# One pool of 80 for the tiles of layer B, and the silu'd gates kept in DRAM

## The chip, the core and the metric

The kernel runs on one core of a Trainium2 chip. The metric is the device time of one execution in microseconds (us), taken as the median of several runs. Besides the times there is one profiled execution, from which the hardware profiler recorded each engine's instructions. The engines are TensorE (PE, with its weight loads shown apart as PEld), VectorE (DVE), ScalarE (ACT), GpSimd (POOL) and SyncE (SP), whose queue issues the DMAs. On-chip memory is SBUF (the working memory, 128 partitions) and PSUM (the accumulators of TensorE).

## What is computed

A trunk of two layers on 512 positions of width 2048, all in float32, and between them a shared key and value side.

```python
def pool_mixer_layer(x, norm_g, w_in, w_group, scale, w_out):      # layer A
    proj = rmsnorm(x, norm_g) @ w_in
    u, gate = proj[..., :W_A], proj[..., W_A:]                     # W_A = 4096, 4 groups
    pooled = [causal_mean_pool(u_g, w) - u_g for w in (2, 4, 8, 16)]
    y = einsum('bsgc,gcd->bsgd', pooled, w_group) * scale * silu(gate)
    return x + y @ w_out

def shared_kv(x, ...):                                             # 512 latents -> 16 heads
    c, k_rope = split(rmsnorm(x, kv_norm_g) @ kv_w_a)
    k_nope, v = split(rmsnorm(c, kv_latent_g) @ kv_w_b)
    return qk_norm_rope([k_nope, k_rope]), v

def mla_layer(x, k, v, ...):                                       # layer B
    q_lat, gate = split(rmsnorm(x, norm_g) @ w_in)                 # gate: 16 heads x 128
    q = qk_norm_rope(rmsnorm(q_lat, q_latent_g) @ w_q_b)
    o = chunk_causal_attention(q, k, v)                            # softmax, causal by chunks of 64
    return x + (o * silu(gate)) @ w_out
```

## The kernel before

The activations are stored transposed: a tile is 128 channels by 512 positions in float32, 2 KB in each partition. To keep float32 accuracy each operand of a product is split into a high part (rounded to the matmul's own format, on ACT) and a low part (the rest, on DVE), and a product is three matmuls, hi x hi, hi x lo and lo x hi (`mm3`, L139 to L143). `load_w` (L114) loads a 128 x 512 weight block from SP's queue into `raw`, and makes `whi` (ACT, L123) and `wlo` (DVE, L124); four of each exist. `proj` (L127) runs one output tile: for 16 inputs, four blocks of weights and 48 matmuls. `split` (L145) makes hi (L146) and lo (L147) of an activation tile.

The stages, in the order of the code:

1. Layer A's input projection, by a scheme of seven products in place of eight (matmuls at L325 to L329). `gather` (L332) adds up the results in a tile `e` and stores them to DRAM scratch (L346, L348). Its memory (the x parts, the weight parts, `e` and small tiles) is given back at the end of the stage.
2. Layer A's rest (L422 to L457). For each of 4 groups `g`: eight pooled tiles, loaded from scratch and split (`pooled_tile`, hi and lo by `at`); eight `y_tile`s (a product with `awg`, hi and lo by `bt`); sixteen products with `awo`, added to the 16 residual tiles `xr` at L455. The residual tiles come from `xt` and are loaded after the y tiles of g = 0 (L450).
3. The norm's gains and the splits of the 16 residual tiles, once for the shared side (`xkv`, from `at`) and once for layer B (`xb`, from `bt`); each residual tile is then spilled to DRAM.
4. The latents: four tiles `cl` from `xt`, the rotary key, the normed `cn` (eight `at` tiles); then the query latents `ql` (four `xt`, evicted from PSUM at L488) and `qn` (eight `at`).
5. The 16 gates, one unit each (`gate_unit`, L568): a `proj` over `xb`, times the norm (L572), then silu into an `at` tile (L574) that is held until its head is done. Gates 0 to 11 come first, then the preparation of head group 0, then gates 12 to 15.
6. The attention, 8 groups of 2 heads. `attn_units` lists a group's work: `score_unit` (matmuls at L731, mask, max at L736, exp at L739), `pt_unit` (transposes of the probabilities, split into `xt` tiles), `pv_unit` (the products with v at L775 to L777, and after a head's second one the gate's product at L780, `V.tensor_tensor(gt, ov, gt, ALU.mult)`). Between them a list of "fill" work is woven, the preparation of the next group, in the order of `PREP`:

```python
PREP = "B k0 k1 k2 k3 K q0 q1 T0 T2 q2 T1 q3 T3 T4 S T5".split()
```

   B loads weights and takes tiles; k0 to k3 are the key and value products (L605 to L607; keys copied at L609); K and S are the statistics of keys and queries (S at L659 to L661 and on); q0 to q3 are the query products (L625 to L627, evicted at L630); T0 to T5 are transposes (L701) followed by splits (T5 ends at L706 and L707, the others in `split`). Due times decide which fill unit stands ahead of which unit of attention (`LEAD`, `PACE`).
7. The output: for the last group, the fill work is `og_unit` (the gated heads are split into `at` or `bt` tiles) and `out_unit` (products with `bwo`). At the end `out_store` loads each spilled tile into an `xt` tile, adds the product and stores the result.

Three pools of SBUF carry the tiles of stages 2 to 7: 32 buffers for `at`, 32 for `bt`, 16 for `xt`, side by side in this order behind the weight buffers. Because `bt` tiles run short in the first head group, its v tiles and two of its transposed pairs are taken from `xt` instead (L591, L710). PSUM has three banks for products (`mm`), two for scores, two for transposes and one for the attention's output. Inside each pool the buffers are handed out in the order of the code; the order in which one engine executes its instructions is chosen by a scheduler, which takes what is ready, and the earlier in the code first.

Of the kernel before, what the change touches and what calls it, by code (L numbers as in the profile page):

```python
# [7 lines left out]
F32 = mybir.dt.float32  # L8
F32R = mybir.dt.float32r
I32 = mybir.dt.int32  # L10
AF = mybir.ActivationFunctionType
# [3 lines left out]
P = 128  # L15
S = 512
# [35 lines left out]
def trunk_kernel(  # L52
# [16 lines left out]
    nc = tc.nc  # L69
    V, A, G, T = nc.vector, nc.scalar, nc.gpsimd, nc.tensor  # L70
# [4 lines left out]
    dpool = ctx.enter_context(tc.tile_pool(name="dpool", bufs=16, space=bass.MemoryType.DRAM))  # L75

    def xt(shape=(P, S), dt=F32):
        return xpool.tile(list(shape), dt, tag="x", name="xt")

    def at(dt=F32R):  # L80
        return apool.tile([P, S], dt, tag="a", name="at")

    def bt(shape=(P, S), dt=F32R):
        return bpool.tile(list(shape), dt, tag="b", name="bt")

    ca = ExitStack()
    tp = [None]
# [1 line left out]
    def tt_(n=S, dt=F32):  # L89
        return tp[0].tile([P, n], dt, tag="t", name="tt_")  # L90
# [4 lines left out]
    def sc():  # L95
        return ps.tile([P, S], F32, tag="sc", name="sc", bufs=2)
# [30 lines left out]
    def proj(w, nk, xs, m=P, acc=None):  # L127

        acc = acc or mm()
        c = S // m if m == P else 4  # L130
        for k0 in range(0, nk, c):
            hi, lo = load_w(w[:, k0 * m:(k0 + c) * m], c * m)
            for j in range(c):
                k = k0 + j
                mm3(acc[:m, :], hi[:, j * m:(j + 1) * m], lo[:, j * m:(j + 1) * m], xs[k],
                    k == 0, k == nk - 1)
        return acc
# [90 lines left out]
    tile_ = dict(reuse_waits="tile")  # L228
# [31 lines left out]
    with ExitStack() as c1:  # L260
# [91 lines left out]
        with ExitStack() as c2:  # L352
            hp = c2.enter_context(tc.tile_pool(name="hp", bufs=2, **tile_))
            for j in range(NJ):
# [11 lines left out]
                a, b = xh[j], xl[j]  # L366
# [43 lines left out]
            gather(ks, pair)  # L410

    wpool = ctx.enter_context(tc.tile_pool(name="wpool", bufs=3, **tile_))
    apool = ctx.enter_context(tc.tile_pool(name="apool", bufs=32, **tile_))
    bpool = ctx.enter_context(tc.tile_pool(name="bpool", bufs=32, **tile_))
    xpool = ctx.enter_context(tc.tile_pool(name="xpool", bufs=16, **tile_))
    tp[0] = ca.enter_context(tc.tile_pool(name="tpool2", bufs=6, **tile_))
    ps = ctx.enter_context(tc.tile_pool(name="ps", bufs=2, space=bass.MemoryType.PSUM, **tile_))

# [3 lines left out]
    def pooled_tile(g, o):  # L422
        x = tt_()
        nc.sync.dma_start(x, raws[g * 8 + o])
        if g:
            x = pool_tile(x, g * 8 + o in neg, WINS[g])
        hi, lo = at(), at()
        split(x, hi, lo)
        return hi, lo

    def y_tile(g, o, pooled):
        z = tt_()
        nc.sync.dma_start(z, raws[32 + g * 8 + o])
        V.scalar_tensor_tensor(z, z, -1.0 if 32 + g * 8 + o in neg else 1.0, ra[0], ALU.mult, ALU.mult)
        A.activation(z, z, AF.Silu)
        acc2 = proj(awg[g, o], 8, pooled)
        c = C_ASC + g * 8 + o
        V.scalar_tensor_tensor(z, acc2, cs[:, c:c + 1], z, ALU.mult, ALU.mult)
        hi, lo = bt(), bt()
        split(z, hi, lo)  # L440
        return hi, lo

    pooled = [pooled_tile(0, o) for o in range(8)]
    for g in range(NG):
        ys = [y_tile(g, o, pooled) for o in range(8)]
        if g == 0:
            rope_tables()
            for k in range(KD):
                x = xt()
                nc.sync.dma_start(x, xT[k])  # L450
                xr.append(x)
        pooled = []
        for o in range(KD):
            acc = proj(awo[g, o], 8, ys)
            V.tensor_tensor(xr[o], xr[o], acc, ALU.add)  # L455
            if g + 1 < NG and o % 2:
                pooled.append(pooled_tile(g + 1, o // 2))  # L457
# [6 lines left out]
    for k in range(KD):  # L464
        hi, lo = at(), at()
        gsplit(xr[k], C_GKV + k, hi, lo)
        xkv.append((hi, lo))
        hi, lo = bt(), bt()
        gsplit(xr[k], C_GB + k, hi, lo)
        xb.append((hi, lo))  # L470
        if k < 2:
            A.activation(accs[k], xr[k], AF.Square)
        else:
            sq = tt_()
            A.activation(sq, xr[k], AF.Square)
            V.tensor_tensor(accs[k % 2], accs[k % 2], sq, ALU.add)
        dsp = dpool.tile([P, S], F32, tag="dsp", name="dsp")
        nc.sync.dma_start(dsp, xr[k])
        spill.append(dsp)
# [10 lines left out]
    def latent_norm(lat, gcol):  # L490
        ac = tt_()
        A.activation(ac, lat[0], AF.Square)
        for o in range(1, 4):
            sq = tt_()
            A.activation(sq, lat[o], AF.Square)
            V.tensor_tensor(ac, ac, sq, ALU.add)
        r = norm_r(ac, 512)
        res = []
        for o in range(4):
            V.scalar_tensor_tensor(lat[o], lat[o], cs[:, gcol + o:gcol + o + 1], r, ALU.mult, ALU.mult)  # L500
            hi, lo = at(), at()
            split(lat[o], hi, lo)
            res.append((hi, lo))
        return res

    cl = []
    for o in range(4):
        c = xt()
        latent(wkvc[o], o, xkv, c)
        cl.append(c)  # L510
# [50 lines left out]
    for o in range(4):  # L561
        c = xt()
        latent(bwin[o], o, xb, c)
        ql.append(c)
    qn = latent_norm(ql, C_GQL)

    gates = []

    def gate_unit(o):
        acc = proj(bwin[4 + o], KD, xb)  # L570
        z = tt_()
        V.tensor_tensor(z, acc, rb[0], ALU.mult)  # L572
        sg = at(F32)
        A.activation(sg, z, AF.Silu)  # L574
        gates.append(sg)


    gqk = const.tile([P, 1], F32, name="gqk")
# [4 lines left out]
    def small(n=8, tag="sm", bufs=6):  # L583
        return spool.tile([P, n], F32, tag=tag, name=tag, bufs=bufs)
# [93 lines left out]
    def tr_unit(hg, u):  # L678

        d = st[hg]  # L680
        if u == 2:


            d["kr"] = []
            for h in range(2):
                p = tr()
                for t in range(4):
                    T.transpose(p[:, t * P:(t + 1) * P], d["krs"][h][:, t * P:(t + 1) * P], ident)
                kh, kl = (xt(dt=F32R) if h else rpool.tile([P, S], F32R, tag="r", name="kr0")), bt()
                split(p, kh, kl)  # L690
                d["kr"].append((kh, kl))
            return
# [25 lines left out]

    def score_unit(hg, h, i):
        d = st[hg]  # L720
        n = (i + 1) * P
        s = sc()
        kh, kl = d[("T", h)]
        krh, krl = d["kr"][h]
        qh, ql_ = d[("T", 3 + h)]
        qr = d["qr"][h]
        qs = slice(i * P, (i + 1) * P)
        ops = [(qh[:, qs], kh[:, 0:n]), (qh[:, qs], kl[:, 0:n]), (ql_[:, qs], kh[:, 0:n]),
               (qr[:, qs], krh[:, 0:n]), (qr[:, qs], krl[:, 0:n])]
        for j, (l, r) in enumerate(ops):  # L730
            T.matmul(s[:, 0:n], l, r, start=(j == 0), stop=(j == 4))  # L731
        V.memset(s[0:64, n - 64:n], -1e30)
        nm = small(1, "nm", 4)
        V.tensor_reduce(nm, s[:, 0:n], AX.X, ALU.max)
        rq = d["rq"][:, 2 * i + h:2 * i + h + 1]
        V.scalar_tensor_tensor(nm, nm, -1.0, rq, ALU.mult, ALU.mult)  # L736
        pe = tt_()
        sm = small(1, "sm", 4)
        A.activation(pe[:, 0:n], s[:, 0:n], AF.Exp, bias=nm, scale=rq, accum_out=sm)  # L739
        V.reciprocal(sm, sm)  # L740
        V.tensor_scalar(pe[:, 0:n], pe[:, 0:n], sm, None, ALU.mult)
        d[("P", h, i)] = pe
# [52 lines left out]
    def attn_units(hg):  # L795
        seq = [(h, i) for h in range(2) for i in range(4)]
        res = []

        for n in range(len(seq) + 2):
            if n < len(seq):  # L800
                res.append(lambda n=n: score_unit(hg, *seq[n]))
            if n >= 2:
                h, i = seq[n - 2]
                res.append(lambda h=h, i=i: pt_unit(hg, h, i))
                if i % 2:
                    res.append(lambda h=h, i=i: pv_unit(hg, h, i // 2))
        return res
# [28 lines left out]
    for o in range(12):  # L836
        gate_unit(o)
    for u in prep_units(0):
        u()
    for o in range(12, NH):  # L840
        gate_unit(o)
# [98 lines left out]
```

## Time and profile before

| what | before |
| --- | --- |
| median of 3 runs | 1957.51 us (1957.45 to 1959.82) |
| profiled execution | 1954.67 us |
| its span, first to last instruction | 1952.5 us |
| mean granted TensorE clock | 0.999 |
| HBM read and written | 208.35 MB, 25.17 MB |

The lines of the profile name an engine, a line of the kernel, an operation and "output <- inputs" by the program's names, with a count of instructions and times in us. "Busy" is the time in which an engine executes something. An idle time in brackets, as in `[0.73 <-ACT whi L123]`, is followed by what ended it: here the ACT instruction at L123 that wrote `whi`. A row of the table by stage gives a stretch of the span, its length, the busy time (and count) of PE, PEld, DVE, ACT and POOL, the clock that TensorE was granted (1.00 is full speed), the share of the DMA engines' time in use, and GB/s.

### The profile page before, as it was taken

To read this page: it belongs to the slowest core of one execution; us is meant where nothing else is said; L and a number is where in the kernel's file an instruction comes from. 1 tells how busy PE (TensorE), PEld (TensorE's weight loads), DVE (VectorE), ACT (ScalarE), POOL (GpSimd) and SP (SyncE) were. 2 spreads that over 40 slices of the span, in tenths; PEclk is the share of its full clock that TensorE was granted. 3 is DMA by queue.
4 is the path that set the end of the run, shared out by engine and by line. 5 is a ranking of instruction groups with operands and counts; after the bars stand their busy time and mean duration, and the time that the engine had idled before them with its cause. 6 is when DMAs were issued, how large, how long until landed. Compare 5 with 4: busy or idle time off the path is not lost.

```text
span 1952.5 us, 30593 instructions
## 1 busy us (share of the span) xinstructions
PE 1920.2 (98%) x11356; PEld 1708.7 (88%) x11356; DVE 1275.8 (65%) x2289; ACT 820.5 (42%) x1561; POOL 264.8 (14%) x404
## 2 busy tenths in 40 slices
PE   8999999999999999999999999999999999999999
PEld 7899999999999878888888888888888888888887
DVE  8766676797666587486695567473344788797432
ACT  7533333333333443333333454332244777785221
POOL 0442323344322100000000000000010111110000
PEclk9999999999999999999999999999999999999999
DMA  6644344335444465334344343333322111121632
GB/s 199 202 135 140 119 138 133 125 125 173 136 124 131 154 212 159 113 121 143 114 130 130 119 146 124 92 92 97 98 92 76 56 39 53 45 70 48 218 119 87
DMA packets 168133, 235.52 MB, mean 121 GB/s; under 512 B 14896, under 2 KB 95152, under 8 KB 167984
## 3 DMA queue, kind: packets, MB, share of 16 engines
q1 hardware_dynamic: 167696, 233.37, 38.0%
q8 instruction: 89, 1.46, 0.3%
q14 instruction: 60, 0.49, 0.1%
q10 hardware_dynamic: 288, 0.20, 0.0%
HBM read 208.35 MB, written 25.17 MB: 120 GB/s over the span
## 4 chain that ended last, share of the span: by engine, by line
PE 91%; DVE 4%; ACT 2%; DMA 1%; issue 1%; SPq 0%; DVEq 0%; ACTq 0%
PE mm L143 16%; PE mm L141 16%; PE mm L142 16%; PE k L329 9%; PE k L325 9%; PE k L327 9%; PE sc L731 2%; PE mm L605 2%; PE mm L607 1%; PE mm L606 1%; PE mm L625 1%; DVE lo L309 1%; PE mm L626 1%; DMA raw<-awin 1%; PE mm L627 1%
## 5 line engine op out<-in xcount | busy, mean ns | idle before, releaser
L123 ACT CAST whi<-raw 128x512 fp32r<-128x512 f32 (+2 forms) x421 | 253.1, 609 | 521.2 <-PE mm L142 451.5
L325 PE MATMUL k<-xh,hi 128*128 128x256 f32 x1680 | 460.0, 283 | 0.0
L327 PE MATMUL k<-xl,hi 128*128 128x256 f32 x1680 | 460.0, 283 | 0.0
L124 DVE TENSOR_TENSOR wlo<-raw,whi 128x512 fp32r<-128x512 f32 (+2 forms) x421 | 281.4, 672 | 231.0 <-ACT whi L123 228.9
L329 PE MATMUL k<-xh,lo 128*128 128x256 f32 x1680 | 418.1, 284 | 4.3 <-DVE lo L309 4.1
L308 ACT CAST hi<-raw 128x1792 fp32r<-128x1792 f32 x120 | 202.8, 1690 | 373.4 <-PE k L329 264.9
L309 DVE TENSOR_TENSOR lo<-raw,hi 128x1792 fp32r<-128x1792 f32 x120 | 248.5, 2071 | 155.7 <-ACT hi L308 155.4
L143 PE MATMUL mm<-bt,wlo 128*128 128x512 f32 x860 | 335.3, 390 | 0.2 <-DVE wlo L124 0.2
L141 PE MATMUL mm<-bt,whi 128*128 128x512 f32 x860 | 334.8, 389 | 0.0
L142 PE MATMUL mm<-bt,whi 128*128 128x512 f32 x860 | 334.5, 389 | 0.0
L327 PEld LDWEIGHTS k<-xl,hi 128*128 128x128 f32 x1680 | 322.5, 192 | 0.0
L325 PEld LDWEIGHTS k<-xh,hi 128*128 128x128 f32 x1680 | 322.5, 192 | 0.0
L329 PEld LDWEIGHTS k<-xh,lo 128*128 128x128 f32 x1680 | 296.7, 192 | 6.0 <-DVE lo L309 5.5
L141 PE MATMUL mm<-at,whi 128*128 128x512 f32 x516 | 201.2, 391 | 3.3 <-ACT whi L123 3.3
L143 PE MATMUL mm<-at,wlo 128*128 128x512 f32 x516 | 202.1, 392 | 1.7 <-DVE wlo L124 1.7
L142 PE MATMUL mm<-at,whi 128*128 128x512 f32 x516 | 202.1, 392 | 0.0
L143 PEld LDWEIGHTS mm<-bt,wlo 128*128 128x128 f32 x860 | 161.4, 188 | 34.6 <-DVE wlo L124 0.6
L141 PEld LDWEIGHTS mm<-bt,whi 128*128 128x128 f32 x860 | 161.4, 188 | 33.7 <-ACT whi L123 0.2
L142 PEld LDWEIGHTS mm<-bt,whi 128*128 128x128 f32 x860 | 161.4, 188 | 33.5
L304 POOL TENSOR_TENSOR raw<-raw 128x256 f32<-128x256 f32 x120 | 102.6, 855 | 430.0 <-DVE raw L302 406.4
L143 PEld LDWEIGHTS mm<-at,wlo 128*128 128x128 f32 x516 | 97.3, 188 | 23.6 <-DVE wlo L124 3.4
L141 PEld LDWEIGHTS mm<-at,whi 128*128 128x128 f32 x516 | 97.1, 188 | 23.6 <-ACT whi L123 3.9
(1174 smaller groups left out, 2584.7 us busy)
## 6 DMA issues: line engine op xcount, KB each, us to landing
raw<-awin SPq DMA_DIRECT2D x240, 256.0 KB, 3.3
raw<-awo SPq DMA_DIRECT2D x128, 256.0 KB, 2.8
raw<-bwin SPq DMA_DIRECT2D x80, 256.0 KB, 2.7
raw<-awg SPq DMA_DIRECT2D x64, 256.0 KB, 2.8
raw<-bwo SPq DMA_DIRECT2D x59, 256.0 KB, 2.8
scr<-e SPq DMA_DIRECT2D x56, 256.0 KB, 2.6
raw<-wkvb SPq DMA_DIRECT2D x32, 256.0 KB, 3.0
raw<-wqb SPq DMA_DIRECT2D x32, 192.0 KB, 2.4
```

The source lines that it names most:

```text
L123: A.copy(hi[:, :n], raw[:, :n])
L124: V.tensor_tensor(lo[:, :n], raw[:, :n], f(hi[:, :n]), ALU.subtract)
L141: T.matmul(dst, wh, xh, start=first, stop=False)
L142: T.matmul(dst, wh, xl, start=False, stop=False)
L143: T.matmul(dst, wl, xh, start=False, stop=last)
L304: G.tensor_tensor(c[:, :, 6, :], c[:, :, 4, :], c[:, :, 2, :], ALU.add)
L308: A.copy(hi, c[:, :, 1:8, :])
L309: V.tensor_tensor(lo, c[:, :, 1:8, :], f(hi), ALU.subtract)
L325: T.matmul(dst, hi[:, j % 2, wi, :], xh[j][:, xi, :], start=first, stop=False, skip_group_check=True)
L327: T.matmul(dst, hi[:, j % 2, wi, :], xl[j][:, xi, :], start=False, stop=False, skip_group_check=True)
L329: T.matmul(dst, lo[:, j % 2, wi, :], xh[j][:, xi, :], start=False, stop=last, skip_group_check=True)
L605: T.matmul(acc, ch[:, tsl], hi, start=(k == 0), stop=False)
```

## The change

All tiles of `xt`, `at` and `bt` come from one pool, `big`, of 80 buffers. A gate is silu'd in place, stored to a DRAM tile, and loaded into an `at` tile at the first score of its head; the product at L780 then uses that tile. The special cases at L591 and L710 stay as they are.

```diff
     def xt(shape=(P, S), dt=F32):
-        return xpool.tile(list(shape), dt, tag="x", name="xt")
+        return big.tile(list(shape), dt, tag="b", name="xt")
     def at(dt=F32R):
-        return apool.tile([P, S], dt, tag="a", name="at")
+        return big.tile([P, S], dt, tag="b", name="at")
     def bt(shape=(P, S), dt=F32R):
-        return bpool.tile(list(shape), dt, tag="b", name="bt")
+        return big.tile(list(shape), dt, tag="b", name="bt")
...
-    apool = ctx.enter_context(tc.tile_pool(name="apool", bufs=32, **tile_))
-    bpool = ctx.enter_context(tc.tile_pool(name="bpool", bufs=32, **tile_))
-    xpool = ctx.enter_context(tc.tile_pool(name="xpool", bufs=16, **tile_))
+    big = ctx.enter_context(tc.tile_pool(name="big", bufs=80, **tile_))
...
         V.tensor_tensor(z, acc, rb[0], ALU.mult)
-        sg = at(F32)
-        A.activation(sg, z, AF.Silu)
-        gates.append(sg)
+        A.activation(z, z, AF.Silu)
+        gd = dpool.tile([P, S], F32, tag="gd", name="gd")
+        nc.sync.dma_start(gd, z)
+        gates.append(gd)
...
     def score_unit(hg, h, i):
         d = st[hg]
+        if i == 0:
+            gt = at(F32)
+            nc.sync.dma_start(gt, gates[2 * hg + h])
+            gates[2 * hg + h] = gt
         n = (i + 1) * P
```

## Prediction

> **What bounds the kernel now.** I read the page's head and its chain of work, then a table of the span by stage, then the timeline at the edges of stages.
>
> ```profile
> span 1952.5 us, 30593 instructions
> PE 1920.2 (98%) x11356; PEld 1708.7 (88%) x11356; DVE 1275.8 (65%) x2289; ACT 820.5 (42%) x1561; POOL 264.8 (14%) x404
> PE 91%; DVE 4%; ACT 2%; DMA 1%; issue 1%; SPq 0%; DVEq 0%; ACTq 0%
> ...
> 660.00:720.00 60.00, 55.48 (x260) 45.50 (x260) 43.90 (x99) 27.15 (x48) 0.33 (x3) 0.97 0.62 211
> 720.00:1240.00 520.00, 520.00 (x2294) 430.25 (x2293) 344.71 (x550) 187.73 (x311) 2.34 (x21) 1.00 0.41 128
> 1300.00:1440.00 140.00, 140.00 (x625) 116.61 (x624) 57.71 (x103) 44.86 (x91) 0.00 (x0) 1.00 0.31 94
> 1440.00:1500.00 60.00, 59.48 (x283) 49.68 (x282) 26.38 (x57) 28.30 (x74) 6.19 (x16) 1.00 0.28 86
> 1500.00:1820.00 320.00, 309.21 (x1798) 270.88 (x1798) 251.49 (x861) 223.85 (x722) 42.77 (x112) 1.00 0.20 63
> ```
>
> The stage rows give a stretch, its length, then busy time of PE, PE's weight loads, DVE, ACT and POOL, granted clock, DMA share, GB/s. TensorE is the bound: it idles 1952.5 - 1920.2 = 32.3 us in all. The change adds and removes no matmul, so it can only move that idle time. Of it 4.5 us lie in 660 to 720 (layer A's first stage gives way to its second), 0.5 in 1440 to 1500, 10.8 in the attention (1500 to 1820), and the rest in stage 1, where no tile of these pools lives, and at the kernel's end. From 720 to 1240 and 1300 to 1440 there is none to win, only some to lose.
>
> **The change part by part.** Joining the pools has one effect that the diff doesn't show. Each pool hands out its buffers in the order of the code, oldest free one first. Three pools are three such lines; one pool is one line, and a tile may not be first written before an earlier one of any kind has been. I therefore looked for places where the trace of before writes an x tile ahead of an a or b tile that the code names earlier, and for places where the new position of a tile meets older memory.
>
> *Gates, off the path.* A gate is now silu'd in place, stored (16 x 256 KB, from SP's queue) and loaded at its head's first score.
>
> ```profile
> L574 ACT ACTIVATE at<-tt__13012 x1: 628/628/628, 1315.9 to 1315.9; 128x512 f32<-128x512 f32 x1
> 1424.38 0.69 DVE L572 TENSOR_TENSOR tt__13859<-mm,r 128x512 f32<-128x512 f32 x1 [1.56 <-PE mm L143]
> raw<-wkvb SPq DMA_DIRECT2D x32, 256.0 KB, 3.0
> L780 DVE TENSOR_TENSOR at<-ov,at x16: 670/686/692, 1539.4 to 1814.0; 128x512 f32<-128x512 f32 x16
> ```
>
> The silu keeps its 0.63 us. The store waits on SP for it; behind it in SP's queue stand the next weight loads, and PE waits for those. A gate is 48 matmuls or 140.0 / 625 x 48 = 10.8 us of PE, with four split weights ahead covering about as much, against 0.69 + 0.63 us from the last matmul to the silu's end. While that prefetch lives, cost 0; without it, some 1.3 us a gate. The 16 stores are 4.2 MB in a stretch whose DMA share is 0.31. The 16 loads take some 3.0 us each and are issued at a head's first score; the product at L780 comes at the head's end. The 16 products stand (1814.0 - 1539.4) / 15 = 18.3 us apart, so a load has some 15 us to spare. Behind a gate load in SP's queue stand the next group's weights, issued long ahead. Cost 0 (bounds -0.5 to +2).
>
> *Layer A's edge (term A).* With one pool of 80 that starts where the a pool did, the first a tiles take position 0 and then those from the top down: they lie on memory where stage 1 still holds its last summed tile e, which two DRAM stores read. In before they lay on the x parts, free earlier.
>
> ```profile
> 667.02 0.62 ACT L146 CAST at<-tt__7458 128x512 fp32r<-128x512 f32 x1
> 669.25 0.50 PE L141 MATMUL mm<-at,whi 128*128 128x512 f32 x1 [2.54 <-ACT whi L123]
> 671.69 0.69 DVE L339 TENSOR_TENSOR e<-e,k 128x512 f32<-128x512 f32 x1
> 672.41 1.17 SPq L348 DMA_DIRECT2D scr<-e  x2
> scr<-e SPq DMA_DIRECT2D x4, 256.0 KB, 3.9
> 669.00:671.00 2.00, 0.73 (x2) 0.30 (x2) 2.00 (x4) 2.00 (x5) 0.00 (x0) 0.92 0.66 149
> 671.00:673.00 2.00, 1.77 (x4) 1.48 (x5) 2.00 (x5) 1.76 (x4) 0.00 (x0) 0.50 0.87 280
> 673.00:675.00 2.00, 2.00 (x8) 1.53 (x8) 2.00 (x4) 0.17 (x1) 0.00 (x0) 0.73 0.96 256
> 675.00:677.00 2.00, 2.00 (x10) 1.65 (x9) 2.00 (x4) 1.48 (x2) 0.00 (x0) 1.00 0.94 334
> 695.20 0.50 PE L141 MATMUL mm<-at,whi 128*128 128x512 f32 x1 [0.73 <-ACT whi L123]
> ```
>
> Before, the splits start at 667.02, while e's last sum (671.69) and its stores (672.41) are still to come. After, the second to fourth pair must wait for the stores: two issues end at 673.6, the later lands 3.9 us from its issue, about 676.9; two splits that leave DVE's line ahead of e's sum may bring that to 675.7, and a split of 0.69 follows: 676.4. Until then PE starts 2 + 4 + 8 + 7 = 21 matmuls in before and could start some 8 after (the first pair's products for two outputs, and the second's high half). 13 matmuls at 520 / 2294 = 0.227 us are 3.0 us. A pause there also meets the clock, which the rows show at 0.50 and 0.73 after the idle from 669 to 671; one more such dip is 2 x 0.5 + 2 x 0.27 = 1.5 us, so 4.5. Against it, the 16 x loads of g = 0 now go out after the y tiles rather than among the group weights (one pool, code order), which relieves the 0.73 us stall at 695.20. The two give 4.5 - 0.7 = 3.8; I take +3.5, bounds +1 (no dip, and one more split in time) and +6 (the stores a store's issue later, no relief). The Trainium skill (TensorE: Matmul & The Clock Gate, Part 1) lets the clock fall only after an idle window of about 3.4 us that runs freely; by that a pause of 2 us alone need not cut it, and A would be 3.0 - 0.7 = 2.3. The trace's dip followed a wait of 2.54 us and 1.27 us of idle in 669 to 671, 3.8 together, so it does not contradict the page.
>
> *Latents (term c).*
>
> ```profile
> 1259.44 0.69 DVE L488 TENSOR_TENSOR xt<-mm,r 128x512 f32<-128x512 f32 x1
> 1281.57 1.89 DVE L147 TENSOR_TENSOR at<-xt,at 128x512 fp32r<-128x512 f32 x3
> 1283.37 0.69 DVE L488 TENSOR_TENSOR xt<-mm,r 128x512 f32<-128x512 f32 x1
> ```
>
> The first two evictions of ql (1259.44 and one 11 us on) ran ahead of the splits of cn, which the code names earlier and which end at 1283.4. Now they wait for them, and hold two of the three accumulation banks. DVE is full there; without two evictions of 0.6 in their way the splits end at 1282.2, and the first eviction, now behind them, at 1282.9. PE's third product, after which it needs that bank, ends between 1281.3 (two products of 10.8 after 1259.44, plus its own lag) and 1283.4 (its eviction in before). A stall of 0 to 1.6; I take +0.9.
>
> *First head group (term d).*
>
> ```profile
> L146 ACT CAST kr<-tr x8: 586/587/591, 1443.5 to 1754.2; 128x512 fp32r<-128x512 f32 x8
> L147 DVE TENSOR_TENSOR bt<-tr,kr x8: 669/671/683, 1479.4 to 1755.4; 128x512 fp32r<-128x512 f32 x8
> ```
>
> The first high half of kr is written at 1443.5, its low half at 1479.4: it waits for a b tile that the last gates' xb still hold. With the 16 gate tiles gone and one pool, that wait ends. The stalls it can return are 0.5 us up to 1500 and 2.1 of the 20 after it: at most -2.6; I take -1.5, since the scores there also wait for the other splits.
>
> *Steady attention (term e).* The tiles of a group are read for the last time well over a hundred instructions before their buffer's turn, so extra buffers release nothing. The single line does bind the order: in code q3's eviction stands after T1's split, in time before it.
>
> ```profile
> 1597.41 0.87 ACT L630 COPY xt<-mm 128x384 f32<-128x384 f32 x2
> 1601.16 0.17 DVE L659 TENSOR_SCALAR qv<-ssq 128x8 f32<-128x8 f32 x1
> 1603.45 0.17 DVE L661 TENSOR_SCALAR qy<-qy 128x8 f32<-128x8 f32 x1
> 1603.65 0.59 ACT L146 CAST bt<-tr 128x512 fp32r<-128x512 f32 x1 [2.52 <-PE tr L701]
> 1604.27 0.69 DVE L147 TENSOR_TENSOR bt<-tr,bt 128x512 fp32r<-128x512 f32 x1 [0.64 <-ACT bt L146]
> 1609.11 0.55 PE L731 MATMUL sc<-bt 128*128 128x128 f32 x3 [0.24 <-ACT tt__16195 L739]
> 1612.12 0.33 PE L731 MATMUL sc<-kr,bt 128*128 128x128 f32 x1 [0.15 <-DVE bt L707]
> ```
>
> The eviction would move from 1597.4 past 1604, and with it the small q statistics on DVE (1601.16 to 1603.62, 2.4 us) into the crowd of splits ahead of the next group's scores at 1609 to 1612, where PE already waits for them. At worst that is 2.4 us in each of 7 groups, +17; at best T1's split moves forward and the wait at its place, 2.52 us on ACT, is used: about -3 over all. DVE's spare time in the stage, (320 - 251.5) / 320 = 21%, and ACT's 30% should take up most; I take a quarter, 0.6 a group, +4.
>
> *Output.* The splits of the gated heads used to run ahead of the last groups' tiles; now they take their turn. That work has spare time of DVE around it: 0 (-2 to +3).
>
> Sum: 3.5 + 0.9 - 1.5 + 4 + 0 + 0 = +6.9, cut to +6, since c may be hidden whole. On the profiled 1954.67 (the span and 2.17 around it) that is 1960.7. The median, 1957.51, stands 2.84 above the profiled time: forecast 1963.5.
>
> **The rivals.** *Faster (0.18).* The repeated gap of the attention is a shortage of buffers, and 16 more dissolve it. Its idle time, 10.8 us, would go, less A's 3.5 and some of e: about -5, 1952.5. For it: the gap comes in every group at the same place. Against it: what PE waits for there is exp and the split of a rotary part, data and not memory. The Trainium skill (Perfetto Trace Analysis, Optimization Strategy) says that consistent bubbles can mean that there is no room for the next tile; the releasers quoted speak for data.
>
> *No change (0.27).* The order of each engine is chosen anew, and finds other work for the moved q statistics: e is 0, A is 2 to 3 and c cancels d: +2, 1959.5. For it: ACT's and DVE's spare time.
>
> *Much slower (0.13).* The crowd ahead of the scores takes all 2.4 us in all 7 groups, 17, and A is 5, c 1.5: +23.5, 1981. It decides from the point at which the q statistics end after 1609. Against it: 9 us of slack from 1603.6 to 1612.
>
> *The change doesn't do what it says:* the single line could be no constraint if buffers went to whoever is ready. Then A remains alone, less d: that is in no change.
>
> **How the numbers follow.** The forecast has 0.42. About 0.2%, 3.9 us, is what a measurement of this kernel can tell; +6 lies close to it, and of the forecast's chance I give 0.06 to no change: faster 0.18, same 0.33, slower 0.49. The range goes from half of the faster rival, 1952, to 1979, just under the much slower one (its lower third within). The forecast's own range is 1959 to 1971.
>
> **What would show it.** Right: on the timeline at 667 to 677 the second pair's split behind the store of e; 660 to 720 with some 8 us of PE idle, not 4.5; the x loads behind the last weights of the y tiles of g = 0; ql's first evictions after cn's splits near 1283; in each group q3's eviction behind T1's split, and the gap before its scores wider than 1 us. Wrong: the attention's idle time well under 10.8 us, or above 20; stalls in 1300 to 1440 behind the gate stores; DVE waiting for a gate load at L780.

## The result, and the profile after

The change makes the kernel slower: 1979.55 us (median of 4 runs, 1978.42 to 1980.89) against 1957.48, a ratio of 1.0117 (95% interval 1.0105 to 1.0129), +22.1 us. The profiled execution took 1980.06 us, 25.4 more than the one of before; its span grew by 25.8.

Line numbers of a view are those of the kernel that ran: the gate's product, L780 before, is L784 in the change and L785 in some of the experiments. The head of the page after, and the chain of work:

```profile
span 1978.3 us, 30646 instructions
PE 1930.6 (98%) x11356; PEld 1717.0 (87%) x11356; DVE 1270.5 (64%) x2289; ACT 822.4 (42%) x1561; POOL 254.6 (13%) x404
PE 91%; DVE 4%; ACT 2%; DMA 2%; issue 1%; SPq 0%; DVEq 0%; ACTq 0%
```

The matmuls are as many as before (11356). Yet PE is busy 10.4 us longer (1930.6 against 1920.2), and idle 15.4 us longer (47.7 against 32.3). So two fifths of the loss is not waiting but the same matmuls at a lower clock (1.0 of the 10.4 us in stage 1, which the change doesn't touch).

The same marks in both traces say where it happens. Stage 2's first matmul starts 1.2 us later (669.25 before, 670.42 after; the change has a stretch of half clock from 91.0 to 94.4 us, early in stage 1, where the code is the same). The gate's product that ends the first head group stands at 1550.22 and at 1557.78 (+7.6), the one that ends the fifth at 1702.19 and 1717.23 (+15.0), the last one at 1814.0 and 1839.6 (+25.6), the end at +25.8. So 6.4 us are lost between layer A's edge and the first group, 7.5 in four steady groups, 10.6 in the last groups, and 0.2 behind them.

The table by stage after (columns as before):

```profile
660.00:720.00 60.00, 55.56 (x264) 46.42 (x264) 43.26 (x94) 25.87 (x47) 0.23 (x2) 0.94 0.42 137
720.00:1240.00 520.00, 516.16 (x2268) 426.10 (x2267) 344.16 (x552) 188.32 (x311) 2.47 (x22) 1.00 0.43 136
1240.00:1300.00 60.00, 59.26 (x261) 47.47 (x260) 35.97 (x74) 20.27 (x43) 0.00 (x0) 1.00 0.31 95
1300.00:1440.00 140.00, 140.00 (x617) 115.58 (x616) 54.87 (x84) 41.99 (x71) 0.00 (x0) 1.00 0.38 115
1500.00:1820.00 320.00, 297.49 (x1705) 261.22 (x1703) 239.16 (x837) 220.24 (x715) 42.11 (x112) 0.97 0.20 62
```

From 1300 to 1440, where the gates are stored, PE has no idle time. From 720 to 1240, where there was none, 3.8 us have come. In the attention (1500 to 1820) it is 22.5 us, where it was 10.8; more than 20 was one of the prediction's signs of being wrong. The waits of PE, longest sums first, with the engine and the instruction that ended them (total us, times, longest); the rows of stage 1 and the wait ahead of stage 2's first matmul, 2.5 us in both kernels, are left out:

```profile
PE tr L754 <- DVE sc L736: 5.8, 6, 1.1
PE mm L141 <- ACT whi L123: 3.8, 1, 3.8
PE ov L779 <- ACT xt L146: 3.3, 7, 0.5
PE sc L735 <- DVE qy L161: 3.2, 1, 3.2
PE tr L754 <- DVE qy L161: 2.4, 4, 0.6
PE mm L142 <- DVE at L147: 2.1, 2, 1.7
```

No row names the load of a gate. In before no wait of the attention sums to more than 1.2 us. `qy` is a q statistic, `whi` a weight's high half, `at` a pooled tile.

**Layer A's edge.** The second pair's low half waits for the stores of e, and PE for it:

```profile
674.49 0.69 DVE L147 TENSOR_TENSOR at<-tt__7458,at 128x512 fp32r<-128x512 f32 x1 [1.10 <-DMA scr<-e]
673.45 0.80 PE L142 MATMUL mm<-at,whi 128*128 128x512 f32 x1 [1.70 <-DVE at L147]
```

**The residual loads.** All 16 now go out in one row of SP's queue, and the weights behind them come too late:

```profile
722.07 9.61 SPq L448 DMA_DIRECT2D xt<-xT  x16
732.07 1.68 SPq L122 DMA_DIRECT2D raw<-awo  x3
739.36 0.64 PE L141 MATMUL mm<-bt,whi 128*128 128x512 f32 x1 [3.84 <-ACT whi L123]
```

In before they stood between the weight loads from 677 to 692, at most seven in one row:

```profile
684.32 4.36 SPq L450 DMA_DIRECT2D xt<-xT  x7
```

**The latents.** The stall of term c is there, by name and by size:

```profile
1290.18 0.47 PE L141 MATMUL mm<-bt,whi 128*128 128x512 f32 x1 [0.74 <-DVE xt L486]
```

**A steady group.** The last of q3's products, then ACT's rows, DVE's and PE's:

```profile
1600.47 0.33 PE L626 MATMUL mm<-wlo,at 128*128 128x384 f32 x1
1612.59 0.59 ACT L146 CAST bt<-tr 128x512 fp32r<-128x512 f32 x1 [2.49 <-PE tr L700]
1613.07 0.49 ACT L629 COPY xt<-mm 128x384 f32<-128x384 f32 x1
1615.56 0.16 DVE L658 TENSOR_SCALAR qv<-ssq 128x8 f32<-128x8 f32 x1
1619.42 0.17 DVE L660 TENSOR_SCALAR qy<-qy 128x8 f32<-128x8 f32 x1
1619.46 0.63 PE L754 MATMUL tr<-cs,tt__15992 128*128 128x128 f32 x4 [0.59 <-DVE qy L161]
1624.43 0.41 PE L754 MATMUL tr<-cs,tt__16121 128*128 128x128 f32 x2 [0.93 <-DVE sc L736]
```

q3's products are done before 1601, and its eviction (1613.07) follows T1's split (1612.59) at once, as forecast; before it stood 6 us ahead of it. The q statistics, 2.5 us in one piece before, now take 4.0, mixed with the work ahead of the scores.

**The last group.** DVE and PE:

```profile
1771.22 0.26 DVE L658 TENSOR_SCALAR qv<-ssq 128x8 f32<-128x8 f32 x1 [0.53 <-ACT junk L632]
1774.62 0.69 PE L735 MATMUL sc<-bt 128*128 128x128 f32 x2 [3.21 <-DVE qy L161]
1784.54 0.68 DVE L147 TENSOR_TENSOR at<-at 128x512 fp32r<-128x512 f32 x1
```

and DVE in before:

```profile
1732.07 0.69 DVE L147 TENSOR_TENSOR at<-at 128x512 fp32r<-128x512 f32 x1
```

These `at<-at` are the splits of the gated heads, on which the output's products depend. Before, they begin at 1732 and PE has those products between the last preparation's chains: from 1740 to 1780 it runs 34 matmuls of L141, which are of the output there. After, the splits stand behind T5's last one (1783.48), PE runs none of these matmuls from 1740 to 1780, and it meets waits of 1.34, 1.21 and 3.21 us.

**The clock.** Stretches of 3.41 us, laid where the granted clock changes; the figure behind the length is PE's busy time, the third from the end the clock. The first row is of before, the others of the change:

```profile
667.26:670.68 3.42, 0.73 (x2) 0.30 (x2) 3.42 (x7) 3.42 (x8) 0.00 (x0) 1.00 0.32 80
671.29:674.70 3.41, 1.71 (x4) 1.06 (x4) 2.31 (x5) 0.00 (x0) 0.00 (x0) 0.50 0.73 220
674.70:678.12 3.42, 3.42 (x9) 2.65 (x9) 2.43 (x5) 2.60 (x5) 0.00 (x0) 0.50 0.88 320
736.14:739.56 3.42, 0.20 (x1) 0.20 (x2) 0.33 (x2) 0.83 (x2) 0.00 (x0) 1.00 0.70 259
739.56:742.97 3.41, 3.41 (x9) 2.45 (x9) 3.08 (x5) 1.02 (x2) 0.11 (x1) 0.50 0.50 136
1661.16:1664.57 3.41, 2.21 (x14) 1.57 (x13) 3.30 (x10) 2.88 (x13) 0.00 (x0) 1.00 0.00 0
1664.57:1667.98 3.41, 3.41 (x9) 2.63 (x8) 2.79 (x11) 3.07 (x13) 0.00 (x0) 0.50 0.07 11
1743.08:1746.49 3.41, 2.21 (x12) 1.58 (x12) 3.33 (x14) 3.38 (x17) 0.00 (x0) 1.00 0.00 0
1746.49:1749.90 3.41, 3.41 (x24) 3.11 (x23) 3.14 (x9) 3.41 (x16) 0.00 (x0) 1.00 0.27 65
1770.38:1773.80 3.42, 1.03 (x7) 0.65 (x5) 2.75 (x16) 1.38 (x6) 1.48 (x4) 1.00 0.00 0
1773.80:1784.04 10.24, 8.73 (x37) 8.05 (x38) 6.63 (x19) 6.47 (x16) 0.00 (x0) 0.50 0.00 0
```

A stretch with much idle time is followed by one at half clock. In before there is one such stretch at layer A's edge (670.68 to 674.09); the change has a second one there. Behind the wait for weights half clock costs another 1.7 us; behind the last group's waits PE is busy 8.73 us at half clock, some 4.4 more than at full clock. In steady groups it goes either way: of two stretches with 2.21 us busy, one was followed by half clock, the other not.

### The profile page after: what moved, and what is told of

Read it like the earlier page. It is cut to its first block, busy times and chain, and to the rows that moved or that the text cites. A ratio compares the mean times of both kernels' runs of the same rounds, so it can differ in the third digit from the quotient of the medians.

```text
span 1978.3 us, 30646 instructions
## 1 busy us (share of the span) xinstructions
PE 1930.6 (98%) x11356; PEld 1717.0 (87%) x11356; DVE 1270.5 (64%) x2289; ACT 822.4 (42%) x1561; POOL 254.6 (13%) x404
## 3 DMA queue, kind: packets, MB, share of 16 engines
q1 hardware_dynamic: 172304, 241.76, 38.9%
## 4 chain that ended last, share of the span: by engine, by line
PE 91%; DVE 4%; ACT 2%; DMA 2%; issue 1%; SPq 0%; DVEq 0%; ACTq 0%
PE mm L142 16%; PE mm L143 16%; PE mm L141 16%; PE k L329 9%; PE k L325 9%; PE k L327 9%; PE sc L735 2%; PE mm L604 2%; PE mm L606 1%; PE mm L605 1%; PE mm L624 1%; PE mm L626 1%; PE mm L625 1%; DVE lo L309 1%; DMA raw<-awin 1%
## 5 line engine op out<-in xcount | busy, mean ns | idle before, releaser
L141 PE MATMUL mm<-bt,whi 128*128 128x512 f32 x860 | 335.7, 390 | 4.6 <-ACT whi L123 3.8
L141 PE MATMUL mm<-at,whi 128*128 128x512 f32 x516 | 202.1, 393 | 2.7 <-ACT at L146 2.5
L141 PEld LDWEIGHTS mm<-bt,whi 128*128 128x128 f32 x860 | 161.8, 188 | 39.1 <-ACT whi L123 5.6
L141 PEld LDWEIGHTS mm<-at,whi 128*128 128x128 f32 x516 | 97.6, 189 | 23.6 <-ACT at L146 2.7
L142 PEld LDWEIGHTS mm<-at,whi 128*128 128x128 f32 x516 | 97.4, 189 | 22.9 <-DVE at L147 2.8
```

Source lines behind the costliest of these rows:

```text
L141: T.matmul(dst, wh, xh, start=first, stop=False)
L142: T.matmul(dst, wh, xl, start=False, stop=False)
```

## The experiments

The theory at this point: one line of hand-outs forces the code's order on tiles that used to pass one another, and this alone makes the loss ("one line"). Its rival: the gates' trip through DRAM. Each kernel ran beside the kernel before on the same chip, so the ratio is what compares; before itself was 1955.8 to 1956.6 us there. Differences between kernels are given below as differences of these ratios, times 1956 us. With the intervals of both, one of less than some 3 to 4 us against the change isn't clear of noise.

**pool_only.** The gates stay on chip:

```diff
-        A.activation(z, z, AF.Silu)
-        gd = dpool.tile([P, S], F32, tag="gd", name="gd")
-        nc.sync.dma_start(gd, z)
-        gates.append(gd)
+        sg = at(F32)
+        A.activation(sg, z, AF.Silu)
+        gates.append(sg)
...
-        if i == 0:
-
-            gt = at(F32)
-            nc.sync.dma_start(gt, gates[2 * hg + h])
-            gates[2 * hg + h] = gt
```

> One pool of 80 as in the change, but the gates stay on chip in their tiles from silu to the product (no store, no load). Theory 'one line' (the loss comes from tiles that must now be handed out in the code's order): all of it is here, 1979.5 us, 1978 to 1981, with the x loads in one burst near 722 us, group periods of 38.9 us and three long waits before the last group's scores. Rival 'gate traffic' (the gate stores and loads, on SP's queue and the DMA engines, cost it): 1957 to 1960.

1981.07 us, ratio 1.0130 (1.0114 to 1.0145).

**gates_only.** The three pools stay, the gates travel (this cut and those below put the edit in short form):

```diff
-    big: 80 buffers
+    apool: 32 buffers for at; bpool: 32 for bt; xpool: 16 for xt
```

> The gates go to DRAM and come back as in the change, but the three pools of before stay apart. Theory 'one line': 1957.5 us, 1956 to 1959, no stall at any load of a gate. Rival 'gate traffic': 1975 to 1980. If both matter, something between, 1962 to 1975.

1957.35 us, 1.0008 (0.9998 to 1.0017). The two settle it: the loss is in the pools, and the gates' stores and loads cost at most 0.2%. In the trace of gates_only no wait of PE is ended by a gate; one steady group takes 39.7 us there, with a wait of 1.21 us for an exp.

**x_apart** and **a_apart.** One kind of tile gets its own line again:

```diff
 x_apart:  big bufs=64 (a and b), xpool bufs=16
 a_apart:  apool bufs=32, big bufs=48 (b and x)
```

> The change, with the x tiles in a pool of 16 of their own; the a and b tiles share one of 64. Theory 'one line': the burst of x loads goes (-6), the latents' stall goes (-0.7), q3's eviction (x) need no longer follow T1's split (b), so the groups take 38.0 us and not 38.9 (-6, and -3 of clock); the splits of the gated heads (a) still follow the last group's b tiles, +9 to +11 against before. Sum 1965 to 1969. Rival 'the groups are longer for another reason than q3 and T1' (the load of the gate, the a and b tiles between them): periods stay at 38.9 and the time is 1972 to 1975.

> The change, with the a tiles in a pool of 32 of their own; the b and x tiles share one of 48. Theory 'one line': the splits of the gated heads run early again as in before, so the three waits before the last group's scores and the clock's fall behind them go (-11), and the edge of layer A too (-1.5); the burst of x loads, the longer groups stay: 1965 to 1969. Rival 'the last group waits for its q statistics because these are late, whatever the splits of the gated heads do': the waits stay at 5 us and more, 1975 to 1979.

x_apart: 1961.21 us, 1.0023 (1.0013 to 1.0032), better than either theory said. a_apart: 1968.25, 1.0068 (1.0052 to 1.0085), as "one line" said. The gate's product that ends a group shows what x_apart did to the groups, which take 37.9 to 38.1 us, as in before:

```profile
1627.00 0.69 DVE L785 TENSOR_TENSOR at<-ov,at 128x512 f32<-128x512 f32 x1 [1.11 <-PE ov L782]
1665.04 0.69 DVE L785 TENSOR_TENSOR at<-ov,at 128x512 f32<-128x512 f32 x1 [1.12 <-PE ov L782]
```

In a_apart the last group's three waits are gone and the residual loads' stall (3.90) and the groups' waits stay. Behind the fifth group's end, where the change loses 10.7 us, x_apart still loses 6.1 and a_apart 0.8. So the groups' loss lies between x and b tiles, the last group's largely between a and b, and the residual loads' between x and b.

**x_spread, q3_first, og_early, all_three.** The pool of 80 stays, and the code's order is altered instead:

```diff
 x_spread:  for o in range(8): y_tile, then two residual loads      (was: 16 behind the eight)
 q3_first:  PREP = "B k0 k1 k2 k3 K q0 q1 T0 T2 q2 q3 T1 T3 T4 S T5"
 og_early:  og_unit(2x), og_unit(2x + 1) behind units k3, K, q0, q1, T0, T2 of the last preparation
 all_three: the three together
```

> The change with one alteration: two of the 16 residual loads stand in the code after each y tile of g = 0, not all 16 after the last. Theory 'code order': the burst near 722 us and the 3.84 us stall with half a window of clock (1.7) behind it go: 1979.5 - 5.5 = 1974, 1972.5 to 1975.5. Rival 'buffers are short' (the loads come late because no buffer is free): unchanged, 1978 to 1981.

> The change with one alteration: in the list of preparation units q3 stands before T1, as the trace of before executed them. Theory 'code order': the q statistics leave the crowd ahead of the scores, group periods fall from 38.9 to 38.0 us (6 groups, -5), the half-clock windows among them go (-3.4): 1971, 1968 to 1973. If the last group's wait for its q statistics goes with it, down to 1963. Rival 'the groups are longer because of the probability tiles or of v's tiles': periods stay near 38.9, 1977 to 1980.

> The change with one alteration: the splits of the first 12 gated heads stand in the code among the units of the last preparation (two heads with each of k3 to T2), not behind it. Theory 'code order': the output's products are ready as fill work while the last group's scores are prepared; the waits of 1.34, 1.21 and 3.21 us go, and the 10.2 us of half clock: -11, 1968.5, 1967 to 1971. Rival 'the last group waits for late q statistics': 1976 to 1980.

> The change with all three alterations at once (residual loads spread, q3 before T1, splits of the gated heads early). Theory 'code order': the whole loss but the edge of layer A and the latents' stall (2.5 together) goes: 1957, 1954 to 1961. Rival 'the single pool costs something of its own besides the order': 1963 and more.

x_spread: 1975.11 us, 1.0100 (1.0085 to 1.0115), -3.3 where -5.5 was expected; the time is hardly clear of noise, but in the trace the stall of 3.84 is gone. og_early: 1971.45, 1.0083 (1.0068 to 1.0098), -6.7 where -11 was expected, the wait of 3.21 gone. q3_first: 1975.84, 1.0106 (1.0091 to 1.0121), -2.2 where -8 was expected, not clear of noise. Its first full period is 38.3 us, the next three are 39.5 with no half clock in them; the change's four are 39.5, 38.9, 40.5 and 40.6, the last two with a stretch of half clock each. all_three: 1966.35, 1.0049 (1.0032 to 1.0065), nine short of the 1957 expected and in the range of the rival "one pool costs something of its own", with periods of 39.5 to 41.1 after the first. The theory holds for two places and fails for the groups: q3 behind T1 isn't their whole cause.

**k_apart, q3_k, all_four.** The next suspect was the copy of the next group's raw keys, which in before passes T5's splits (1609.09 against 1610.78):

```diff
 k_apart:   big bufs=76, kpool bufs=4 for d["kraw"];  q3_k: q3_first too;  all_four: all_three too
```

> The change with four of the 80 buffers set aside for the raw keys alone, so that the copies of the next group's keys need not follow the last splits of this one (T5); q3 still follows T1. Theory 'two inversions in the groups, q3 behind T1 and the keys behind T5': half of the groups' loss goes, periods of 38.4 to 38.6 us, 1976, 1973 to 1978. Rival 'the keys do not matter': periods stay at 38.9, 1978 to 1981. Rival 'only the keys matter': 38.0, 1970 to 1973.

> The change with both: q3 ahead of T1 in the list, and four buffers of their own for the raw keys. Theory 'two inversions': periods fall to 38.0 us, the half-clock windows of the groups go, 1970, 1967 to 1973; the burst of residual loads and the last group's late splits stay. Rival 'the probability tiles, too, are out of order': periods of 38.5 and more, 1973 to 1977.

> The change with all four orders repaired: residual loads spread, q3 ahead of T1, raw keys apart, splits of the gated heads early. Theory 'code order': what is left is the edge of layer A with a second window of half clock (3) and the latents' stall (1): 1960, 1957 to 1963. Rival 'one pool costs something of its own': 1965 and more.

k_apart: 1974.22 us, 1.0099 (1.0085 to 1.0112), but with periods still at 38.9 and more: the gain of its trace is in the last groups. q3_k: 1984.3, 1.0146 (1.0132 to 1.0160), worse than the change, with 39.6 to 41.9. all_four: 1970.41, 1.0077 (1.0064 to 1.0091), far from the 1960 expected and in the range of "one pool costs something of its own". "Two inversions" falls: freeing these two, while the probability tiles stay in the line, doesn't shorten the groups. What one pool costs of its own, if not this order, these runs don't tell; back_p below shows what the probability tiles alone cost.

**x_og.** x tiles apart, and og_early; the two changes whose effect was plain:

> The change with the x tiles in a pool of 16 of their own and the splits of the first 12 gated heads early in the code; the a and b tiles share one pool of 64. Theory 'code order': all that it lost is repaired, 1956.5, 1954 to 1959, within 0.2% of before. Rival 'the last group still waits': 1960 to 1964, as with the x tiles apart alone.

1953.3 us (11 runs, 1950.91 to 1954.98), ratio 0.9987 (0.9978 to 0.9996), just below the range expected. All that the change lost is back, and the kernel is faster than both others, than before by 0.13%, an interval that leaves out no change by little. Against x_apart, which has the same pools, the early splits gave 7 us. With the splits of the gated heads in their early place,

```profile
1733.78 0.69 DVE L147 TENSOR_TENSOR at<-at 128x512 fp32r<-128x512 f32 x1
```

the last group's longest wait of a score is 0.48 us, where the kernel before has 1.09.

**back_q, back_k, back_p.** In x_og all x tiles are free. Each of these puts one kind back into the line of a and b tiles, with no size changed:

```diff
 back_q:  q            -> big        back_k:  d["kraw"]  -> big        back_p:  d["pth"], d["ptl"]  -> big
```

> The repaired kernel (x tiles apart, splits of the gated heads early) with one kind of x tile put back into the line of the a and b tiles: the raw queries. Theory 'every x tile that has to wait for a b tile costs': q3 follows T1, group periods 38.3 to 38.6, 1953.3 + 3 = 1956, 1955 to 1959. Theory 'q3 behind T1 is the whole of the groups' loss', as the prediction had it: periods 38.9, 1959 to 1963. Rival 'the queries don't matter': 1952 to 1954.5.

> The repaired kernel with the raw keys alone put back into the line of the a and b tiles. The keys' copies then follow T5's splits. Theory 'every x tile': 38.3 to 38.6, 1956, 1955 to 1960. Theory 'q3 alone': periods stay at 38.0, 1952 to 1954.5.

> The repaired kernel with the probability tiles alone put back into the line of the a and b tiles. T4's and T5's splits and the probabilities' splits then bind each other. Theory 'every x tile': 38.5 to 39.0, since there are twelve such tiles in a group, 1958, 1955 to 1962. Theory 'q3 alone': 1952 to 1954.5.

back_q: 1957.75 us, 1.0010 (1.0001 to 1.0020). back_k: 1955.89, 1.0000 (0.9991 to 1.0010). back_p: 1961.22, 1.0031 (1.0019 to 1.0043). Against x_og's 0.9987 that is +4.5, +2.5 and +8.6 us; the 2.5 is only just clear of the two intervals. Periods, by two products of back_q, two of back_k and three of back_p:

```profile
1669.65 0.69 DVE L785 TENSOR_TENSOR at<-ov,at 128x512 f32<-128x512 f32 x1 [1.00 <-PE ov L782]
1708.08 0.69 DVE L785 TENSOR_TENSOR at<-ov,at 128x512 f32<-128x512 f32 x1 [0.90 <-PE ov L782]
```
```profile
1627.87 0.69 DVE L785 TENSOR_TENSOR at<-ov,at 128x512 f32<-128x512 f32 x1 [0.70 <-PE ov L782]
1666.53 0.69 DVE L785 TENSOR_TENSOR at<-ov,at 128x512 f32<-128x512 f32 x1 [0.70 <-PE ov L782]
```
```profile
1628.93 0.69 DVE L785 TENSOR_TENSOR at<-ov,at 128x512 f32<-128x512 f32 x1 [0.82 <-PE ov L782]
1668.66 0.69 DVE L785 TENSOR_TENSOR at<-ov,at 128x512 f32<-128x512 f32 x1 [0.96 <-PE ov L782]
1707.06 0.69 DVE L785 TENSOR_TENSOR at<-ov,at 128x512 f32<-128x512 f32 x1 [0.87 <-PE ov L782]
```

Those are 38.43 us, 38.66, and 39.73 and 38.40. The mean of four periods is 38.0 in before and in x_og. It is 38.9 in back_q (38.5 without a stretch of half clock in its first period), 38.7 in back_k, and 39.2 in back_p, whose four take 40.1, 38.4, 39.7 and 38.4 with no half clock in them. In the change it is 39.9, or 39.0 without its two stretches of half clock. So every kind of x tile costs by itself, the queries 0.5 and the keys 0.7 a group, and the probability tiles 1.1, about as much as all x tiles together in the change (1.0): the costs don't add up. "q3 alone" is refuted by back_k and back_p.

**swap_pools.** Only the places of x_og's two pools are exchanged:

```diff
-    big: 64 buffers, then xpool: 16
+    xpool: 16 buffers, then big: 64
```

> The repaired kernel with the places of its two pools exchanged, so that the top of the a and b tiles' pool lies where stage 1 keeps its last e tile; no order in the code is changed. Theory of the edge: the second pair of pooled tiles waits for e's stores, a second window of half clock follows: +1.6 to +3.5, 1955 to 1957. Rival 'the place in memory does not matter': 1952 to 1954.5.

1955.95 us, 1.0000 (0.9991 to 1.0010), +2.5 against x_og's ratio, again only just clear of the intervals, and the edge's two lines come back:

```profile
675.11 0.69 DVE L147 TENSOR_TENSOR at<-tt__7461,at 128x512 fp32r<-128x512 f32 x1 [1.20 <-DMA scr<-e]
673.97 0.80 PE L142 MATMUL mm<-at,whi 128*128 128x512 f32 x1 [1.84 <-DVE at L147]
```

The place in memory alone makes this wait; x_og has none for e. The second stretch of half clock behind it isn't the wait's alone. back_k, whose pools lie as in x_og and where nothing waits for e, has one there too:

```profile
672.01:675.42 3.41, 2.67 (x6) 2.15 (x7) 3.41 (x7) 2.44 (x5) 0.00 (x0) 0.50 0.85 239
675.42:678.84 3.42, 3.42 (x9) 2.64 (x8) 3.42 (x7) 2.46 (x4) 0.00 (x0) 0.50 0.99 316
```

So not all of the 2.5 us need come from the place.

## Why the prediction was wrong

The direction and the cause, one line of hand-outs, were right. The size was not: +6 forecast, +22.1 measured, just past the range's end at 1979. What each term became can be read from the profiled executions, by how much later than in before the same matmul, counted from the start of stage 2, or the same product of a gate stands: 1.2 us for the first matmul, 3.1 for the 20th, 1.5 for the 120th, 7.4 for the 300th, 8.4 for the products of the first twelve gates (the twelfth at 1432.80, 1424.38 before), 7.6 at the end of the first head group.

- *Gates, 0:* right (gates_only; no row of a wait for a gate).
- *Edge, +3.5:* right in mechanism and too dear. The wait is 1.70 us with a second stretch of half clock behind it, 1.9 us by the 20th matmul; by the 120th the relief has given 1.6 back, where 0.7 was booked, so +0.3 is left. PE idles 4.4 us from 660 to 720, as before, and not the 8 that were named as a sign of being right. The clock was misread, too: the wait of 2.54 us and the idle 1.27 us, summed to 3.8, overlap, and in the stretch ahead of the half clock PE was busy 0.73 us, so it was no idle window.
- *Residual loads:* wrong in sign, +6.0. The prediction saw that they move behind the y tiles and booked only what they leave behind. It didn't ask what they meet at their new place: 16 issues take SP 9.61 us, the weights of the first output products queue behind them, and a stall of 3.84 us and half clock follow. In x_spread's trace the stall is gone.
- *Latents, +0.9:* right, a wait of 0.74 and 1.0 from mark to mark.
- *First head group, -1.5:* right in sign, -0.9.
- *Steady attention, +4 (0.6 a group):* the place was right and the price low: 0.9 to 1.6 a group without half clock and 2.5 with a stretch of it, 7.5 us in four groups. The named cause was one of three: the raw keys and the probabilities pass b tiles too (back_k, back_p).
- *Output, 0 (-2 to +3):* the largest miss, 10.6 in the last groups; og_early gave 6.7 us back. "That work has spare time of DVE around it" looked at the engine that does the splits, not at who waits for them: the output's products are PE's fill work in the last group. This is the step that failed, with the residual loads.
- *Clock:* counted once, at the edge, with 1.5 us. Over the kernel it is 10.4 us of longer busy time, all but 1.0 of it within the terms above. Half clock at the residual loads, in the steady groups and in the last groups was left out.

With the 1.2 us of stage 1, which the change doesn't touch, the measured terms add up to 25.7 of the 25.8 us between the profiled executions.

The rival of 1981 named nearly the right time for a wrong reason: its crowd ahead of the scores was to cost 2.4 us in each of 7 groups, and the queries alone cost 0.5 (back_q). The faster rival's shortage of buffers isn't borne out: with 16 buffers more for a, b or x tiles (gates_only, and the change itself) no gap closed. The number of buffers alone was never varied, though.

What stays open: why q3_first and q3_k don't shorten the groups at full clock, and q3_k even makes them longer than the change does. Each has a new order of all engines, and the runs tell that freeing part of the x tiles is no step toward freeing all, not by what rule. Nor was the early place of the splits tried with the three pools of before, so the 0.13% that x_og is faster has no cause shown.

## What to carry to other kernels

A pool is a queue as well as memory: tiles from one pool are handed out in the code's order, so before joining pools, list the places where the trace shows a tile of one pool written ahead of an earlier one of the other, and price each at its new place: what it meets there, and whom its consumer feeds. Work that fills a bound engine's gaps is on the path even if the engine that makes it is half idle. Where pools must be joined, keep the tiles that run early in a pool of their own, or move their code to where the trace executes it. The second paid here for the splits of the gated heads and took away the residual loads' stall, and failed inside the groups; the x tiles apart and the early splits made the joined a and b pool as fast as the three.

## What the runs showed of the hardware

The granted clock changes on a grid of 3.41 us: in each of the 18 traces the edges of half clock lie whole multiples of 3.41 us apart, and a stretch of half clock lasts one, two or three of them (3.41, 6.83 or 10.24 us). The grid doesn't start with the kernel: laid back to the start of the span, it has a remainder of 1.67 us in before and of 2.28 in the change. A stretch need not be idle to cost the next one half its clock. In the change, PE's busy time in the stretch ahead was 0.20, 1.03 and 2.21 us of 3.41 where half clock followed, and 2.21 too where it didn't. Over all 18 traces, a stretch at full clock with less than 1.5 us busy was always followed by half clock, and one with more than 2.3 us never; between these it went either way. The steady groups' 2.21 lie in that band. The Trainium skill (TensorE: Matmul & The Clock Gate, Part 1) has the length of the window and that it runs freely, and the trace agrees; by its rule of an idle window the stretches with 1.03 and 2.21 us busy would not have been followed by half clock, and the trace decides against that.

One kernel's time scatters along with the clock: x_spread ran between 1971.66 us (mean clock 0.996) and 1978.10 (0.994). The 0.002 are some 4 of these 6.4 us. That the same waits met the grid at another place there is likely and not shown, since only one execution has a trace.
